# One query tile moved forward, and four smaller reorderings, in a two-layer hybrid decoder trunk

## The chip, the core and the metric

The kernel runs on one core of a Trainium2 chip. The metric is the device time of one execution in microseconds. The core has TensorE (PE, matrix products into PSUM banks), VectorE (DVE), ScalarE (ACT), GpSimd (POOL) and SyncE (SP), and DMA engines that are started from the queues of SP, ACT and POOL. Each engine works through its own instructions in order and waits on semaphores.

## The reference

A residual stream of 16 learned meta tokens and 512 tokens (528 columns, 1024 channels, float32) passes two layers. Per layer:

```
h = rmsnorm(x) * gain
u, z_pool, c_q, c_kv, k_rope, z_mla, g_pool, g_mla = split(h @ w_in)     # 512,512,768,256,32,512,1024,1024
y_pool = (pool_mix(u, w_group) * pool_scale * silu(z_pool)) @ pool_w_up  # causal means over 2,4,8,16 tokens, minus u
y_mla  = (attention(c_q, c_kv, k_rope) * silu(z_mla)) @ mla_w_up         # 8 heads, 64+32 wide, q/k norms, rotary part
x = x + (sigmoid(g_pool) * y_pool + sigmoid(g_mla) * y_mla) @ w_out
```

The meta columns are dropped from the output, so in the last layer most products run on 512 columns, in the first on 528 in two halves of 264.

## The kernel before

**Products.** All activations lie channel-major (channels on partitions, tokens in columns). Each float32 product is made of three reduced-precision ones: a weight tile `w` is split into `whi` (a ScalarE copy, L187) and `wlo` (a VectorE subtraction, L188), the activation into `hh` and `hl`, and `mm3` (L192, L195, L196) adds `whi*hh`, `whi*hl` and `wlo*hh` in one PSUM bank. There are four banks tagged `mm`, three tagged `S` and one `o`.

**The stream of products.** `register` writes down, layer by layer, the list `plan` of `Gemm`s; `stream` walks it in pieces of 512 weight columns (four 128-wide steps of the contraction). At each piece it asks `wload` for the next piece's weights: a DMA from SP's queue into `raw` (three buffers), then the two splits into rings of three (or, for tiles marked `spare`, two other buffers). When an output tile is complete its evacuation function (`ev_cq`, `ev_u`, `ev_o`, ...) takes it out of PSUM. The attention heads and norms are written between the pieces: `go` calls `fill`, `fill_now`, `upto`, which step the stream on by a modelled time (`clk`) or to a named product. `behind(a, b)` adds a dependency: `a` may not start before `b` has ended. `newest[0]` is the matmul last written down, `earlier(ns)` the one written `ns` nanoseconds of the modelled clock ago. The framework's scheduler then orders each engine's instructions by its own simulated timeline, so the order in the queues is near that of the program, but not the same.

**The order in a layer.** ckv0, ckv1 (key/value latent), then the norm's sums and its reciprocal root, which goes to memory and comes back broadcast as `inv` (`rinv<-ndr`). Meanwhile cq0 to cq4 run (query latent; they need no `inv`, `ev_cq` only sums squares into `racc` on POOL). Then u0, k0, u1, kr, k1, u2, k2, u3, k3 (pooled inputs and keys; `ev_u` and `ev_k` multiply by `inv` or `cinv`), v, then `yw`: the 512 columns of the pooled group weights, kept in two `sv` buffers for the four products y0 to y3. The rest alternates zp (pool gate) with y tiles as fillers: zp0, zp1, y0, zp2, y1, zp3, y2, cq5, y3; then qr0, qr1 (rope part of the queries, with a rotation on VectorE and POOL in `rope`), qn0 to qn3, pu, zm, the gates and the heads. `qr` and `qn` need all six cq tiles.

**Output.** After the products mu0 to mu7 the residual stream is read back into `xb` by eight DMAs of POOL (`residual`). o0, o1, o2 and o3 are plain products with w_out, 128 output channels each; `ev_o` adds half of the PSUM bank to `xb` on VectorE (L1092) and starts the tile's write (`out`, L1101; in the last layer to `yT`, from POOL's queue). The other four output tiles are computed in pairs with seven instead of eight half products, a Strassen-like scheme (`out_pairs`): group `oa` holds products 1, 2, 7, 6, 5 for two pairs, o3 follows, then group `ob` holds 4 and 3. VectorE prepares sums and differences of the activations (`blend`); sums of weight tiles were made in memory long before by plain and accumulating DMAs (`weight_sums`, L356 and L359). Some products are added to two outputs: `carry` (L1163, L1164) copies the bank to a buffer on ScalarE and adds it to `xb` by an accumulating DMA of POOL; the next product for the same bank accumulates on it, so it waits for that copy.

Of the kernel before, what the change touches and what calls it, by code (L numbers as in the profile page):

```python
# [10 lines left out]
F32R = mybir.dt.float32r  # L11
BF16 = mybir.dt.bfloat16
I32 = mybir.dt.int32
AF = mybir.ActivationFunctionType
ALU = mybir.AluOpType
# [7 lines left out]
NM = 16  # L23
# [49 lines left out]
def trunk(ctx, tc, xT, pos, win, wkr, wqb, wkb, wvb, wgr, wpu, wmu, wout, gains, const, yT):  # L73
# [17 lines left out]
    def slot(tag, dt=F32, bufs=1, w=W):  # L91
        return sl.tile([P, w], dt, tag=tag, name=nm(tag), bufs=bufs)

    def tmp(w=W):
        return tp.tile([P, w], F32, tag="tmp", name=nm("tmp"), bufs=3)
# [18 lines left out]
    def fetch(src, n, raw, eng):  # L114
        eng.dma_start(raw[:, :n], src)
        return raw

    def rawt():
        return wp.tile([P, 512], F32, tag="raw", name=nm("raw"), bufs=3)
# [49 lines left out]
            return self.src[c // 512] if isinstance(self.src, list) else self.src[:, c:c + n]  # L169

    loads = [0]

    def wload(src, n, gain, spare, buf=None, held=False):
        raw = early.pop(0) if early else fetch(src, n, buf or rawt(), sp)
        loads[0] += 1
        pool, th, tl, nb = (tp, "th", "tl", 2) if loads[0] <= 2 or spare else (wp, "whi", "wlo", 3)
        if gain is not None:
            v = raw[:, :n].rearrange("p (k m) -> p k m", k=8)
            gp.tensor_mul(v, v, gain.unsqueeze(2).to_broadcast([P, 8, n // 8]))
            return raw, None  # L180
        if held:
            hi, lo = slot("sv", F32R, bufs=2), slot("sv", F32R, bufs=2)
            split(hi, lo, raw[:, :n], 0, n)
            return hi, lo
        hi = pool.tile([P, W if pool is tp else 512], F32R, tag=th, name=nm("whi"), bufs=nb)
        lo = pool.tile([P, W if pool is tp else 512], F32R, tag=tl, name=nm("wlo"), bufs=nb)
        act.activation(hi[:, :n], raw[:, :n], AF.Copy)  # L187
        dve.tensor_sub(lo[:, :n], raw[:, :n], hi[:, :n].bitcast(F32))  # L188
        return hi, lo

# [10 lines left out]
    def earlier(ns):  # L201
        return next((m for c, m in reversed(past) if c <= clk[0] - ns), past[0][1])

    newest = [None]
    plan = []
# [96 lines left out]
    def split(hi, lo, src, a, b):  # L302
        act.activation(hi[:, a:b], src, AF.Copy)  # L303
        dve.tensor_sub(lo[:, a:b], src, hi[:, a:b].bitcast(F32))  # L304

    def behind(ins, other):
        tc.add_manual_dep(ins.ins, other.ins.name,
                          mybir.DependencyInfo(mybir.DependencyClass.Sync, mybir.DependencyReason.DATA))
# [38 lines left out]
    def weight_sums(name, w):  # L347
        def made(u, i):
            a, b = w[2 * u], w[2 * u + 1]
            d = wsum[name][u]  # L350
            src = {0: (b[:, 0:512], b[:, 512:1024]), 2: (a[:, 0:512], b[:, 0:512]), 1: (a[:, 0:512], d[:, 0, :]),
                   3: (a[:, 512:1024], d[:, 1, :])}
            return d[:, i, :], src[i]

        def copy(d, src):
            behind(sp.dma_start(d, src[0]), earlier(14000))  # L356

        def add(d, src):
            behind(gp.dma_start(d, src[1], accum_op=ALU.add), earlier(4000))  # L359

        for u in range(len(w) // 2):
            for fn, i in ((copy, 0), (copy, 2), (add, 0), (copy, 1), (add, 2), (add, 1), (copy, 3), (add, 3)):
                yield lambda fn=fn, u=u, i=i: fn(*made(u, i))

    class Layer:
# [723 lines left out]
        def ev_o(self, m, nxt):  # L1089
            def ev(ps, a, b):  # L1090
                x = xb[:, m, a:b]
                dve.scalar_tensor_tensor(out=x, in0=ps, scalar=0.5, in1=x, op0=ALU.mult, op1=ALU.add)  # L1092
                self.out(m, (a, b), nxt, gp)
                if not self.last and m == 3 and b == T:
                    nxt.square_x(m)
            return ev
# [46 lines left out]
        def out_pairs(self, nxt, name, products):  # L1143
            order = [(p, u) for p in products for u in range(2)]
            l = self.l
            a, b, c = self.halves()
            n = b - a
            A, B = (a, b), (b, c)
            src = []
            for p, u in order:  # L1150
                w0, w1 = wout[l, OUT[2 * u]], wout[l, OUT[2 * u + 1]]
                src.append({1: w0[:, 0:512], 2: w0[:, 512:1024], 4: w1[:, 512:1024]}.get(p))
                if src[-1] is None:
                    src[-1] = wsum[l][u][:, {5: 0, 6: 1, 7: 2, 3: 3}[p], :]
            bank = self.banks

            def grow(m, s, v):
                x = xb[:, m, s[0]:s[1]]
                dve.scalar_tensor_tensor(out=x, in0=v, scalar=0.5, in1=x, op0=ALU.mult, op1=ALU.add)

            def carry(m, s, v, u, scale, o):
                t = self.carried[u][:, o:o + n]
                act.activation(t, v, AF.Copy, scale=scale)  # L1163
                gp.dma_start(xb[:, m, s[0]:s[1]], t, accum_op=ALU.add)  # L1164

            def body(i, w):
                p, u = order[i]
                m0, m1 = OUT[2 * u:2 * u + 2]
                key = {2: "e", 7: "c", 4: "c"}.get(p, "a"), u
                if key not in bank:  # L1170
                    bank[key] = (sct if key[0] == "a" else mmt)()
                ps = bank[key][:, :n]
                t, o = (B if p == 3 else A), (0 if p == 1 else 4)
                for k in range(4):
                    xh, xl = (x[:, t[0]:t[1]] for x in self.mg[k + o]) if p < 4 else self.tt[k][p]
                    c_ = P * k
                    mm3(ps, w[0][:, c_:c_ + P], w[1][:, c_:c_ + P], xh, xl, k == 0 and p in (1, 2, 7), k == 3, True)
                    if k == 1:
                        yield 6 * (n / 2.4)
                q = sp if name == "ob" else gp  # L1180
                if p == 1:
                    self.carried[u] = slot("sv", bufs=2)
                    carry(m0, A, ps, u, 0.5, 0)
                elif p == 2:
                    grow(m0, A, ps)
                    self.out(m0, A, nxt, q)
                elif p == 7:
                    grow(m1, B, ps)
                elif p == 6:
                    carry(m1, A, ps, u, -0.5, HALF)  # L1190
                elif p == 5:
                    carry(m1, B, ps, u, -0.5, 0)
                    self.out(m1, B, nxt, q)
                    if u == 1 and not self.last:
                        for m in range(3):
                            nxt.square_x(m)
                elif p == 4:
                    grow(m1, A, ps)
                    self.out(m1, A, nxt, q)
                else:  # L1200
                    grow(m0, B, ps)
                    self.out(m0, B, nxt, q)
                    if not self.last:
                        nxt.square_x(m0)
                        nxt.square_x(m1)
                if i == len(order) - 1:
                    done.add((l, name))
                yield 6 * (n / 2.4)

            plan.append(Gemm((l, name), src, 512 * len(src), body=body))  # L1210
            plan[-1].more = True

        def register(self, nxt):
# [4 lines left out]
            def add(name, src, width, **kw):  # L1218
                plan.append(Gemm((l, name), src, width, **kw))
# [5 lines left out]
            def cq(m):  # L1225
                add(f"cq{m}", wi(MT_CQ + m), D, evac=self.ev_cq(m), xs=hs, segs=XS)
# [1 line left out]
            def kk(p):  # L1228
                add(f"k{p}", wkb[l, p], 256, evac=self.ev_k(p), xs=cs, segs=FULL)

            for m in range(5):
                cq(m)
            for m in range(4):
                add(f"u{m}", wi(MT_U + m), D, evac=self.ev_u(m), xs=hs, segs=FULL)
                if m == 1:
                    add("kr", wkr[l], 256, body=self.kr_body, gain=gn[:, l * N_GAIN + G_H:l * N_GAIN + G_H + 8])
                kk(m)
# [4 lines left out]
                add(f"y{m}", None, P, body=self.y_body(m))  # L1242

            add("v", wvb[l], 1024, body=self.v_body)
            add("yw", wgr[l], 512, body=self.hold)
            plan[-1].held = True
            zp(0)
            zp(1)
            y(0)
# [1 line left out]
            y(1)  # L1251
            zp(3)
            y(2)
            cq(5)
            y(3)
            for r in range(2):
                add(f"qr{r}", wqb[l, r], 768, evac=self.ev_qr(r), xs=lambda: self.cqs, segs=XS)
            for p in range(4):
                add(f"qn{p}", wqb[l, 2 + p], 768, evac=self.ev_qn(p), xs=lambda: self.cqs, segs=XS)
            for m in range(8):  # L1260
# [17 lines left out]
                add(f"mu{m}", wmu[l, m], 512, evac=self.ev_mu(m), xs=lambda: self.ogs, segs=XS)  # L1278
                plan[-1].spare = m % 2 == 1
            mg = lambda: self.mg  # L1280
            self.banks, self.carried = {}, {}
            for m in range(4):
                if m == 3:
                    self.out_pairs(nxt, "oa", (1, 2, 7, 6, 5))
# [165 lines left out]
```

## Time and profile before

| | |
|---|---|
| median of three runs | 781.85 us (781.79 to 782.32) |
| profiled execution | 781.9 us |
| its span, first to last instruction | 780.1 us |
| TensorE busy | 773.2 us, 5469 matmuls, full clock |
| VectorE busy | 569.7 us |
| ScalarE busy | 444.7 us |
| POOL busy | 232.7 us |

The span is 1.8 us shorter than the profiled execution's own time. A row of a timeline gives start and duration in microseconds, engine, source line, operation, output and inputs by the program's names, shape, count, and in brackets the engine's idle time before it with what ended it. A matmul's shown duration is longer than the step to the next start, because matmuls overlap. A row of a stage (from:to, its length) gives busy microseconds with instruction counts for PE, its weight loads, DVE, ACT and POOL, then the granted clock, the share of the 16 DMA engines and GB/s. A row of DMA issues gives target, source, queue, count, size and the median time from issue to landing.

### The profile page before, as it was taken

To read this page: it belongs to the slowest core of one execution; us is meant where nothing else is said; L and a number is where in the kernel's file an instruction comes from. 1 tells how busy PE (TensorE), PEld (TensorE's weight loads), DVE (VectorE), ACT (ScalarE), POOL (GpSimd) and SP (SyncE) were. 2 spreads that over 40 slices of the span, in tenths; PEclk is the share of its full clock that TensorE was granted. 3 is DMA by queue.
4 is the path that set the end of the run, shared out by engine and by line. 5 is a ranking of instruction groups with operands and counts; after the bars stand their busy time and mean duration, and the time that the engine had idled before them with its cause. 6 is when DMAs were issued, how large, how long until landed. Compare 5 with 4: busy or idle time off the path is not lost.

```text
span 780.1 us, 15325 instructions
## 1 busy us (share of the span) xinstructions
PE 773.2 (99%) x5469; PEld 710.9 (91%) x5469; DVE 569.7 (73%) x1326; ACT 444.7 (57%) x1016; POOL 232.7 (30%) x303
## 2 busy tenths in 40 slices
PE   9999999999999999999999999999999999999998
PEld 8999899999999999999997898887788999988887
DVE  5848787446778876589764577866897888864994
ACT  7645555645566665645564446546657766664552
POOL 1024525103335333211330136221006625340213
PEclk9999999999999999999999999999999999999999
DMA  6232457765646465565662424425557666662645
GB/s 245 82 96 89 125 171 151 177 168 144 156 110 164 116 141 120 156 156 184 169 171 82 109 75 122 133 62 178 146 132 167 173 187 158 175 226 72 210 137 154
DMA packets 65325, 112.92 MB, mean 145 GB/s; under 512 B 10704, under 2 KB 15696, under 8 KB 65248
## 3 DMA queue, kind: packets, MB, share of 16 engines
q1 hardware_dynamic: 55344, 92.18, 39.1%
q0 software_dynamic: 8896, 17.92, 12.9%
q10 hardware_dynamic: 1008, 1.84, 0.7%
q8 instruction: 43, 0.70, 0.4%
q14 instruction: 34, 0.28, 0.1%
HBM read 100.18 MB, written 22.62 MB: 157 GB/s over the span
## 4 chain that ended last, share of the span: by engine, by line
PE 91%; DVE 4%; DMA 2%; ACT 1%; issue 1%; POOL 0%; DVEq 0%; ACTq 0%; POOLq 0%
PE mm L192 26%; PE mm L196 26%; PE mm L195 25%; PE S L195 3%; PE S L196 3%; PE S L192 3%; PE mm L979 2%; DVE wlo L188 1%; PE o L985 1%; PE o L984 1%; PE S L506 1%; DMA raw<-wgr 1%; DMA xb<-xT 1%; PE mm L408 1%; ACT whi L187 0%
## 5 line engine op out<-in xcount | busy, mean ns | idle before, releaser
L192 PE MATMUL mm<-hh,whi 128*128 128x264 f32 (+2 forms) x992 | 306.2, 311 | 0.5 <-DVE u L550 0.4
L196 PE MATMUL mm<-hh,wlo 128*128 128x264 f32 (+2 forms) x992 | 304.4, 309 | 0.1
L195 PE MATMUL mm<-hl,whi 128*128 128x264 f32 (+2 forms) x992 | 304.1, 308 | 0.0
L188 DVE TENSOR_TENSOR wlo<-raw,whi 128x512 fp32r<-128x512 f32 (+1 forms) x253 | 180.0, 714 | 100.3 <-ACT whi L187 98.0
L187 ACT ACTIVATE whi<-raw 128x512 fp32r<-128x512 f32 (+1 forms) x253 | 154.2, 613 | 168.7 <-PE mm L195 110.2
L192 PEld LDWEIGHTS mm<-hh,whi 128*128 128x128 f32 x992 | 186.2, 188 | 11.3 <-issue 1.0
L195 PEld LDWEIGHTS mm<-hl,whi 128*128 128x128 f32 x992 | 186.8, 188 | 8.7
L196 PEld LDWEIGHTS mm<-hh,wlo 128*128 128x128 f32 x992 | 185.9, 188 | 9.0 <-DVE wlo L188 0.6
L922 POOL TENSOR_SCALAR pa<-pa,rs 128x272 f32<-128x272 f32 (+1 forms) x32 | 33.2, 1038 | 103.3 <-DVE rs L941 64.5
L922 POOL TENSOR_SCALAR cq<-cq,rs 128x400 f32<-128x400 f32 (+1 forms) x32 | 51.2, 1600 | 0.0
L192 PE MATMUL mm<-cq,whi 128*128 128x264 f32 (+2 forms) x140 | 43.8, 313 | 0.0
L195 PE MATMUL mm<-cq,whi 128*128 128x264 f32 (+2 forms) x140 | 43.7, 312 | 0.0
L196 PE MATMUL mm<-cq,wlo 128*128 128x264 f32 (+2 forms) x140 | 43.3, 312 | 0.1
L908 DVE CUSTOM_DVE_ANT_0 S<-S,maskw,nqs 128x272 f32<-128x272 f32 (+4 forms) x80 | 38.6, 498 | 5.3 <-PE S L196 5.0
L725 POOL TENSOR_TENSOR racc<-racc,tmp 128x264 f32<-128x264 f32 (+1 forms) x15 | 14.0, 936 | 85.5 <-ACT tmp L724 85.5
L304 DVE TENSOR_TENSOR tl<-mm,th 128x512 fp32r<-128x512 f32 (+1 forms) x64 | 30.0, 483 | 8.0 <-ACT th L303 6.3
L359 POOL DMA_DIRECT2D wsum<-wout x8 | 7.0, 875 | 91.6 <-PE mm L196 86.9
L303 ACT ACTIVATE th<-mm 128x512 fp32r<-128x512 f32 (+1 forms) x64 | 26.3, 433 | 10.2 <-PE mm L979 9.6
L915 ACT ACTIVATE cq<-S,bia 128x400 f32<-128x400 f32 (+2 forms) x48 | 24.5, 514 | 13.2 <-DVE bia L953 8.5
L192 PE MATMUL mm<-u,whi 128*128 128x264 f32 (+1 forms) x96 | 31.3, 326 | 0.0
L196 PE MATMUL mm<-u,wlo 128*128 128x264 f32 (+1 forms) x96 | 30.9, 322 | 0.0
L195 PE MATMUL mm<-kn,whi 128*128 128x264 f32 (+1 forms) x96 | 30.6, 320 | 0.0
(344 smaller groups left out, 1684.7 us busy)
## 6 DMA issues: line engine op xcount, KB each, us to landing
raw<-win SPq DMA_DIRECT2D x139, 256.0 KB, 2.8
raw<-wout SPq DMA_DIRECT2D x22, 256.0 KB, 3.6
bc<-kdr SPq DMA_DIRECT2D x16, 264.0 KB, 4.5
wsum<-wout SPq DMA_DIRECT2D x16, 256.0 KB, 3.5
raw<-wpu SPq DMA_DIRECT2D x16, 256.0 KB, 2.7
wsumgp<-win SPq DMA_DIRECT2D x16, 256.0 KB, 3.4
raw<-wmu SPq DMA_DIRECT2D x16, 256.0 KB, 2.8
raw<-wsumgp SPq DMA_DIRECT2D x16, 256.0 KB, 4.3
```

The costliest lines, as they stand in the source:

```text
L187: act.activation(hi[:, :n], raw[:, :n], AF.Copy)
L188: dve.tensor_sub(lo[:, :n], raw[:, :n], hi[:, :n].bitcast(F32))
L192: first = pe.matmul(out, wh, xh, start=start, stop=False, skip_group_check=more)
L195: pe.matmul(out, wh, xl, start=False, stop=False, skip_group_check=more)
L196: newest[0] = pe.matmul(out, wl, xh, start=False, stop=stop, skip_group_check=more)
L303: act.activation(hi[:, a:b], src, AF.Copy)
L304: dve.tensor_sub(lo[:, a:b], src, hi[:, a:b].bitcast(F32))
L725: self.acc_last = gp.tensor_add(self.acc[:, a:b], self.acc[:, a:b], t[:, :b - a])
L908: dve.tensor_tensor_reduce(out=sv, in0=sv, in1=mask, scale=nqs[:, i, h:h + 1], scalar=3e38, op0=ALU.add, op1=ALU.min, accum_out=bia[:, c:c ...
L915: act.activation(pv, sv, AF.Exp, scale=-1.0, bias=bia[:, i:i + 1], accum_out=rs[:, c:c + 1])
L922: gp.tensor_scalar(pt[i], pt[i], rs[:, i:i + 1], None, op0=ALU.mult)
L979: pe.transpose(tr[:, P * (i - j):P * (i - j + 1)], pt[i][:, NM + P * j:NM + P * (j + 1)], ident)
```

## The change

Five edits in one:

1. `register`: cq5 goes in front of u0, behind cq4. Its former place between y2 and y3 is taken by qr0; qr1 follows y3.
2. `register` and `wload`: `yw` goes from behind v to behind u2 (ahead of k2). Its load takes a buffer of the tag `bc` (three, otherwise used by the heads for broadcast rows) in place of one of the three `raw` buffers, and waits for the matmul last written down.
3. `wload` and `carry`: a ScalarE split of a weight tile that is the second or third one written down after a `carry` may not start before that carry's copy.
4. `ev_o` in the last layer, for o0, o1 and o2: in place of the VectorE addition, a ScalarE copy with factor 0.5 into a `tmp` buffer and an accumulating DMA of POOL into `xb`. The write to `yT` is put off: it is written down after the first product of group `ob`, on SP's queue, behind that product's last matmul.
5. `weight_sums`: the accumulating DMAs wait for a matmul 9000 ns back on the modelled clock, not 4000.

```
 loads = [0]
+urgent = []

 def wload(src, n, gain, spare, buf=None, held=False):
+    if held:
+        hi, lo = slot("sv", F32R, bufs=2), slot("sv", F32R, bufs=2)
+        raw = slot("bc", bufs=3)
+        behind(sp.dma_start(raw[:, :n], src), newest[0])
+        split(hi, lo, raw[:, :n], 0, n)
+        return hi, lo
     raw = early.pop(0) if early else fetch(src, n, buf or rawt(), sp)
...
-    if held:
-        hi, lo = slot("sv", F32R, bufs=2), slot("sv", F32R, bufs=2)
-        split(hi, lo, raw[:, :n], 0, n)
-        return hi, lo
...
-    act.activation(hi[:, :n], raw[:, :n], AF.Copy)
+    made = act.activation(hi[:, :n], raw[:, :n], AF.Copy)
+    for e in urgent:
+        e[1] += 1
+        if 1 < e[1] < 4:
+            behind(made, e[0])
     dve.tensor_sub(lo[:, :n], raw[:, :n], hi[:, :n].bitcast(F32))

 def add(d, src):                                  # in weight_sums
-    behind(gp.dma_start(d, src[1], accum_op=ALU.add), earlier(4000))
+    behind(gp.dma_start(d, src[1], accum_op=ALU.add), earlier(9000))

 def ev(ps, a, b):                                 # in ev_o
     x = xb[:, m, a:b]
+    if self.last and m < 3:
+        t = tmp()[:, a:b]
+        act.activation(t, ps, AF.Copy, scale=0.5)
+        gp.dma_start(x, t, accum_op=ALU.add)
+        self.later.append(lambda: behind(sp.dma_start(yT[:, m, a - NM:b - NM], x), newest[0]))
+        return
     dve.scalar_tensor_tensor(out=x, in0=ps, scalar=0.5, in1=x, op0=ALU.mult, op1=ALU.add)

 def carry(m, s, v, u, scale, o):                  # in out_pairs
-    act.activation(t, v, AF.Copy, scale=scale)
+    urgent.append([act.activation(t, v, AF.Copy, scale=scale), 0])
     gp.dma_start(xb[:, m, s[0]:s[1]], t, accum_op=ALU.add)
...
+    while self.later and name == "ob":            # in body, after the product's additions
+        self.later.pop(0)()

-for m in range(5):                                # in register
+for m in range(6):
     cq(m)
 for m in range(4):
     add(f"u{m}", ...)
+    if m == 2:
+        add("yw", wgr[l], 512, body=self.hold)
+        plan[-1].held = True
     if m == 1:
         add("kr", ...)
     kk(m)
...
 add("v", wvb[l], 1024, body=self.v_body)
-add("yw", wgr[l], 512, body=self.hold)
-plan[-1].held = True
...
 y(2)
-cq(5)
+qr(0)
 y(3)
-for r in range(2):
-    add(f"qr{r}", ...)
+qr(1)
```

More of the change, by code (lines that the diff above doesn't have):

```diff
@@ L1253, in register, with qr @@
             y(2)
-            cq(5)
-            y(3)
-            for r in range(2):
-                add(f"qr{r}", wqb[l, r], 768, evac=self.ev_qr(r), xs=lambda: self.cqs, segs=XS)
+            def qr(r):
+                add(f"qr{r}", wqb[l, r], 768, evac=self.ev_qr(r), xs=lambda: self.cqs, segs=XS)
+            qr(0)
+            y(3)
+            qr(1)
             for p in range(4):
@@ L1280, in register @@
             mg = lambda: self.mg
-            self.banks, self.carried = {}, {}
+            self.banks, self.carried, self.later = {}, {}, []
             for m in range(4):
```

## The prediction

> **What bounds the kernel now.** I read the page's head, then the work by stage (busy microseconds of each engine in a stretch, instruction counts in brackets, granted clock, DMA share and GB/s).
>
> ```profile
> span 780.1 us, 15325 instructions
> PE 773.2 (99%) x5469; PEld 710.9 (91%) x5469; DVE 569.7 (73%) x1326; ACT 444.7 (57%) x1016; POOL 232.7 (30%) x303
> 75.00:90.00 15.00, 14.59 (x104) 12.72 (x106) 12.70 (x25) 9.69 (x24) 13.05 (x12) 1.00 0.43 141
> 720.00:757.00 37.00, 36.01 (x180) 30.08 (x178) 35.11 (x72) 19.91 (x42) 5.51 (x10) 1.00 0.51 164
> 772.70:777.40 4.70, 4.21 (x36) 4.00 (x35) 1.70 (x4) 0.00 (x0) 1.08 (x2) 1.00 0.66 196
> ```
>
> TensorE (PE) is busy 773.2 of 780.1 us at full clock, and the change neither adds nor removes a matmul. So nothing that makes another engine faster counts by itself: the end can only move by the holes in TensorE's stream, or by what follows its last matmul. Holes are read from the timeline of PE by the step from one start to the next, since a matmul's shown duration overlaps its successor.
>
> ```profile
> 57.97 0.28 PE L195 MATMUL mm<-kl,whi 128*128 128x264 f32 x1
> 58.09 0.28 PE L196 MATMUL mm<-kh,wlo 128*128 128x264 f32 x1
> 58.80 0.36 PE L192 MATMUL mm<-hh,whi 128*128 128x264 f32 x1 [0.42 <-DVE u L550]
> 83.35 0.39 PE L195 MATMUL mm<-wlo,kh 128*128 128x512 f32 x1
> 83.58 0.40 PE L196 MATMUL mm<-whi,kl 128*128 128x512 f32 x1
> 84.38 0.50 PE L192 MATMUL mm<-whi,kh 128*128 128x512 f32 x1 [0.41 <-DVE u L550]
> 476.03 0.40 PE L196 MATMUL mm<-whi,kl 128*128 128x512 f32 x1
> 476.48 0.50 PE L192 MATMUL mm<-whi,kh 128*128 128x512 f32 x1
> 531.85 0.40 PE L195 MATMUL mm<-cq,whi 128*128 128x512 f32 x1
> 532.33 0.50 PE L196 MATMUL mm<-cq,wlo 128*128 128x512 f32 x1
> 755.73 0.28 PE L196 MATMUL mm<-hh,wlo 128*128 128x256 f32 x1
> 757.08 0.39 PE L192 MATMUL S<-cq,whi 128*128 128x256 f32 x1 [1.07 <-ACT sv L1163]
> ```
>
> An undisturbed step is 0.12 us for 264 columns (57.97 to 58.09) and 0.23 for 512 (83.35 to 83.58); for 256 columns I also use 0.12. The holes are then 0.71 - 0.12 = 0.59 us at 58, 0.80 - 0.23 = 0.57 at 84, 0.45 - 0.23 = 0.22 at 476, 0.48 - 0.23 = 0.25 at 532, and 1.35 - 0.12 = 1.23 at 756. All five lie in stages that the change touches. The first four edits reach the holes at 58, 84, 476 and 756: 0.59 + 0.57 + 0.22 + 1.23 = 2.61 us is what they can win there.
>
> **The sixth query-latent tile (cq5) before u0.** Who made the hole at 58? SyncE's queue and the engines behind it:
>
> ```profile
> 42.15 0.37 SPq L115 DMA_DIRECT2D raw<-win  x1
> 49.03 0.33 SPq L444 DMA_DIRECT2D rinv<-ndr  x1
> ndr<-ny SPq DMA_DIRECT2D x4, 2.0 KB, 8.4
> 52.54 0.63 ACT L187 ACTIVATE whi<-raw 128x512 fp32r<-128x512 f32 x1 [5.10 <-DMA raw<-win]
> 57.41 0.90 DVE L188 TENSOR_TENSOR wlo<-raw,whi 128x512 fp32r<-128x512 f32 x1 [1.04 <-ACT whi L187]
> 58.23 0.76 DVE L550 TENSOR_TENSOR u<-mm,rinv 128x264 f32<-128x264 f32 x2
> ```
>
> The norm row goes to memory and back, and its four scattered writes take 8.4 us to land. SyncE stands until 49.03 behind them, and the weight tile issued at 42.15 reaches ScalarE only at 52.54, after 5.10 us of idleness. From then on ScalarE and VectorE work off cq4's evacuation and the splits late, and u0's evacuation at 58.23 sits behind a split: TensorE wants u0's PSUM bank for u1 after the short k0. This backlog made the hole. With cq5 in front, 48 more matmuls, 48 x 0.12 = 5.8 us, stand between the late tile and u0; they need cq4's banks no sooner than u0 did, and only cq5 follows, not a short k tile. I take the whole 0.59 as won. What covers the delayed group (all of u, k, kr, v moves back by 5.8 us) is that same tile; nothing outside waits for it before the heads. In the second layer no hole stands at this place, so I count nothing there.
>
> Between y2 and y3 the place of cq5 goes to qr0 (18 matmuls a column half, against 24), so y3 comes nearer to its pooled input; but in layer one y3's operand (window 3) is made long before, and qr0's operands are now old. I cost the filler itself at nothing. What it does to VectorE is below.
>
> **The pooled weights (yw) early, through buffers of their own.** The holes at 84 and 476 have one cause:
>
> ```profile
> 79.42 0.33 SPq L115 DMA_DIRECT2D raw<-wgr  x1
> 82.32 0.63 ACT L303 ACTIVATE sv<-raw 128x512 fp32r<-128x512 f32 x1 [2.28 <-DMA raw<-wgr]
> 82.98 1.00 DVE L304 TENSOR_TENSOR sv<-raw,sv 128x512 fp32r<-128x512 f32 x1 [0.85 <-ACT sv L303]
> 83.91 0.42 DVE L550 TENSOR_TENSOR u<-mm,rinv 128x264 f32<-128x264 f32 x1
> ```
>
> ScalarE waits 2.28 us for this load, VectorE another 0.85 behind ScalarE, and u3's evacuation, next in VectorE's order, frees the bank only after 83.91. After the change the load needs no free buffer of the ring of three; it starts after a matmul in the middle of u2 and lands, by the same 2.9 us (79.42 to 82.32), about when u2's second half ends. The split can still hold ScalarE and VectorE for a moment, but what is then late is k2's bank, which is wanted only a whole u tile later (5.8 us). SyncE's queue is passed by one wait on a matmul; behind it are the weights for k2 and u3, two buffers ahead. I take 0.57 + 0.22 as won, at worst half of it.
>
> **The last layer's o0 to o2, and the order of the splits behind the carries.** The hole at 756:
>
> ```profile
> 750.66 0.68 DVE L1092 SCALAR_TENSOR_TENSOR xb<-mm,xb 128x512 f32<-128x512 f32 x1
> 755.42 0.68 DVE L188 TENSOR_TENSOR wlo<-raw,whi 128x512 fp32r<-128x512 f32 x1
> 756.12 0.63 ACT L187 ACTIVATE whi<-raw 128x512 fp32r<-128x512 f32 x1 [1.57 <-PE mm L196]
> 756.66 0.64 ACT L1163 ACTIVATE sv<-S 128x256 f32<-128x256 f32 x2
> xb<-sv POOLq DMA_DIRECT2D x6, 128.0 KB, 3.5
> yT<-xb POOLq DMA_DIRECT2D x4, 256.0 KB, 3.4
> ```
>
> Both carries (756.66) were behind a split that ScalarE waited 1.57 us to start; TensorE needed them, because the next product accumulates on the bank they read. VectorE is full here (35.11 of 37.00 us in the stage), so the splits of the pair products are late too. The change takes three 0.68 us additions off VectorE (2.04 us) and gives ScalarE, busy 19.91 of 37.00, three copies of about 0.63 (the row of a 512-wide ScalarE pass). It also lets the second and third split after a carry start only behind it. Upper end: all 1.23. Lower end: the split of 756.12 ends at 756.75, and its product cannot start before: 757.08 - 756.75 = 0.33 is then all there is. I take 1.0, near the upper end, since VectorE's 2.04 us come before that split's raw buffer was freed. In layer one the carry edit meets no hole; I cost it at nothing, as a split is made two to three chunks ahead, each of 12 matmuls of 0.12 us.
>
> The three additions become accumulating DMAs of 256 KB; half that size takes 3.5 us to land, and nobody reads these tiles until the end, 20 us on. Three writes of the result move from POOL's queue to SyncE's, behind the first product of the last group, at about 773: 768 KB more in the last 4.7 us, where the DMA engines now are at 0.66 and 196 GB/s. At that share the stage could carry 196 / 0.66 = 297 GB/s, an estimate, so 0.34 x 4.7 x 297 = 0.47 MB fit into the idle share and 0.3 MB, about 1.0 us, do not. Bounds 0 and 1.0; I take 0.1, because the last write's issue is the latest of all and most of the excess has drained by the landing. [...]
>
> **The weight sums (9000 for 4000).** Each accumulating DMA of the sums waits for a matmul some 5 us older. POOL issues them sooner and blocks less; the copy it needs waits for a matmul 14000 ns back and is written down two tasks before it. No hole lies there. Nothing, plus or minus 0.1.
>
> **qr0, y3, qr1 on VectorE.** In layer two the hole at 532 comes from VectorE beside POOL's rope:
>
> ```profile
> 512.00 0.43 DVE L188 TENSOR_TENSOR wlo<-raw,whi 128x256 fp32r<-128x256 f32 x1 [0.40 <-ACT whi L187]
> 517.70 1.25 DVE L304 TENSOR_TENSOR tl<-tmp,u 128x512 fp32r<-128x512 f32 x1 [0.70 <-ACT u L303]
> 528.44 1.53 DVE L188 TENSOR_TENSOR wlo<-raw,whi 128x256 fp32r<-128x256 f32 x1
> 527.88 1.81 POOL L541 TENSOR_TENSOR q<-q,tc 128x512 f32<-128x512 f32 x1 [1.29 <-DVE tmp L835]
> ```
>
> The same 256-wide split takes 0.43 us with POOL idle and 1.53 with the rope running. y3's evacuation (a 512-wide pass of 0.68 and the split, 1.25 beside POOL) now falls between two ropes: 1.9 us of VectorE against y3's three matmuls of 0.23. Bounds: the hole of 0.25 goes (y3 parts the ropes), or 1.9 - 0.7 = 1.2 us come on top. I take 0.1 lost: most of these operations have no near deadline.
>
> Sum: 0.59 + 0.57 + 0.22 + 1.0 - 0.1 - 0.1 = 2.18 us. The profiled execution took 781.9 us (its span of 780.1 and 1.8 around it), the median of the runs is 781.85; the forecast is 781.9 - 2.2 = **779.7 us**. A difference of 0.2%, 1.56 us, is about what a measurement of this kernel can tell from no change.
>
> **Rivals.** *The end hole stays.* For it: ScalarE's split at 756.12 waits on TensorE, and the weights behind it are loaded only when VectorE frees raw buffers. Then 0.33 is won in place of 1.0, and the tail may cost up to 1.0: 2.18 - 0.67 = 1.5 without the tail, 0.6 with it, so 780.4 to 781.3. Against: VectorE's relief. No measurable change.
>
> *VectorE and POOL collide around qr0.* 1.2 us lost for 0.1 gives 2.18 - 1.1 = 1.1 won, 780.8 us; if layer one, where no hole stands now, pays the same again, nothing is won: 781.9. [...]
>
> *Slower: SyncE's queue stops in the last group.* The three result writes wait for the first product of the last group; in the program's order the loads of its third and fourth weight tiles come after them.
>
> ```profile
> 764.94 0.33 SPq L115 DMA_DIRECT2D raw<-wsum  x1
> 773.41 4.32 SPq L1101 DMA_DIRECT2D yT<-xb  x4
> ```
>
> If the load of 764.94 came behind them, at about 773.4, then with 3.4 us to land (as the 256 KB write above) and 0.63 + 0.68 of splitting its product would start at 778.1. Now the last write's issue ends at 773.41 + 4.32 = 777.73, some 0.8 us behind the last product, and two products of 12 x 0.12 = 1.44 us end there, so the third starts at about 774.1: 4.0 us lost, and with the 2.2 won 783.7 us. It decides only if the load stands behind the writes. Against: now, too, this load precedes a write (773.41) that the program issues before it, so SyncE's order goes by readiness. A new order elsewhere with holes of that size belongs to the same case.
>
> *The change does not do what it says*: the splits and loads keep their order and 781.9 stays; part of the second case.
>
> **How the numbers follow.** Forecast case 0.62, its own range 778.6 (2.61, the 0.25 at 532, and some 0.1 us for each of the four slow first matmuls after a hole, such as 0.50 for 0.39) to 780.3. End hole stays 0.13 and collision or no effect 0.12, up to 781.9: within 0.2% together 0.25. Slower 0.13. The range 778.6 to 782.0 leaves out the slower case and little else.
>
> **What would show it.** Right: no step over 0.2 us before the matmul that follows k0, none in v's first products, and the first S product of group oa within 0.4 us of its predecessor; ScalarE's wait for wgr under 0.5 us. Wrong: a wait of SyncE before the last raw load, a split of over 1.5 us between qr0 and qn0 with a hole behind it, or over 3.2 us from the last addition's end to the end of the span.

## The result, and the profile after

The changed kernel took 786.6 us (median of 13 runs, 782.55 to 788.54); the kernel before, beside it, 782.62 us (13 runs, 781.72 to 783.95). The ratio is 1.0041, with a 95% interval of 1.0029 to 1.0052: 0.4% slower, where 0.3% faster was forecast. The changed kernel's times spread more than those of before, and with TensorE's mean granted clock: three runs at 1.000 took 782.55 to 783.69 us, the ten at 0.997 to 0.999 took 784.32 to 788.54. The profiled execution took 786.6 us.

The head of the page and the work by stage of the changed kernel. The first stage is that of the prediction, with 5 us more for the work that now comes later; the second holds the work that lay at 720 to 757 before, 4.0 us later now:

```profile
span 784.4 us, 15328 instructions
PE 774.5 (99%) x5469; PEld 712.3 (91%) x5469; DVE 568.7 (73%) x1323; ACT 446.5 (57%) x1019; POOL 229.4 (29%) x303
75.00:95.00 20.00, 20.00 (x152) 18.20 (x152) 18.60 (x38) 12.31 (x30) 13.85 (x13) 1.00 0.35 109
724.00:761.00 37.00, 36.88 (x183) 30.45 (x182) 34.45 (x71) 20.81 (x45) 8.09 (x13) 1.00 0.59 166
```

The span is 4.3 us longer. In the early stage TensorE now has no gap (20.00 of 20.00), and in the second VectorE has 34.45 us of work for 35.11: 0.7 less, not 2.04, since other work has come in. The holes that the prediction named look like this now (timeline of PE, start and shown duration):

```profile
64.04 0.28 PE L203 MATMUL mm<-kh,wlo 128*128 128x264 f32 x1
64.16 0.28 PE L199 MATMUL mm<-hh,whi 128*128 128x264 f32 x1
89.05 0.40 PE L203 MATMUL mm<-whi,kl 128*128 128x512 f32 x1
89.28 0.39 PE L199 MATMUL mm<-whi,kh 128*128 128x512 f32 x1
758.23 0.28 PE L203 MATMUL mm<-hh,wlo 128*128 128x256 f32 x1
758.61 0.39 PE L199 MATMUL mm<-hh,whi 128*128 128x256 f32 x1
764.78 0.28 PE L202 MATMUL S<-u,whi 128*128 128x256 f32 x1
765.33 0.38 PE L203 MATMUL S<-cq,wlo 128*128 128x256 f32 x1 [0.27 <-DVE wlo L195]
```

Behind k0 the step to u1 is 0.12 us, in v's first products 0.23: those holes are gone, as are the ones at 476 and 532. The hole of 1.23 at 756 has become 0.38 - 0.12 = 0.26 us, one of 0.17 right behind it, and 0.55 - 0.12 = 0.43. So of the five holes that the prediction read four are gone, and of the fifth 0.37 us is won where 1.0 was forecast. The loss is elsewhere, in layer one, ahead of the products mu, where the prediction had not looked:

```profile
332.75 0.28 PE L203 MATMUL mm<-hh,wlo 128*128 128x264 f32 x1
335.93 0.51 PE L199 MATMUL mm<-q,whi 128*128 128x264 f32 x2 [2.90 <-ACT q L310]
337.25 0.42 PE L199 MATMUL mm<-q,whi 128*128 128x264 f32 x1
337.46 0.42 PE L202 MATMUL mm<-kn,whi 128*128 128x264 f32 x1
332.77 1.15 ACT L190 ACTIVATE whi<-raw 128x512 fp32r<-128x512 f32 x2 [3.66 <-DMA raw<-wmu]
333.43 1.29 DVE L195 TENSOR_TENSOR wlo<-raw,whi 128x512 fp32r<-128x512 f32 x2 [3.60 <-ACT whi L190]
328.00:336.00 8.00, 5.10 (x42) 4.84 (x40) 3.49 (x10) 2.74 (x9) 0.00 (x0) 1.00 0.57 133
336.00:340.00 4.00, 4.00 (x21) 4.00 (x22) 2.76 (x11) 1.77 (x5) 0.00 (x0) 0.57 0.48 151
```

Read from the bracket backwards: TensorE stood for 2.90 us, because ScalarE stood for 3.66 us until a load of mu's weights landed, and VectorE for 3.60 behind ScalarE; the operands of the next products stand in their queues behind the splits of those weights. The step is 3.18 us, 3.06 of it lost. Behind the hole the granted clock is 0.57 on average over 4 us, and a matmul step is 0.21 to 0.23 us in place of 0.12: another 0.43 x 4 = 1.7 us. These 4.8 us and some smaller holes, less what was won, are the longer span. The largest of the smaller ones are new too, in layer two (0.46 us at 668.6 and 0.80 at 670), and begin in the same way, with ScalarE behind a load (in the kernel before it stood 0.48 us at this place):

```profile
667.90 0.63 ACT L190 ACTIVATE whi<-raw 128x512 fp32r<-128x512 f32 x1 [2.29 <-DMA raw<-win]
```

The load for which ScalarE stood in layer one, on the chain of work that ended last, before and after (start, then time to landing):

```profile
328.35 2.55 DMA raw<-wmu
327.30 5.38 DMA raw<-wmu
```

It takes 2.83 us longer, which is what the hole has grown by (3.06 for 0.23 at 333.8 before). What delays it is seen in POOL's queue, before (L359) and after (L366), from the second of three in a row:

```profile
329.27 0.81 POOL L359 DMA_DIRECT2D wsumgp<-win  x1 [8.68 <-PE mm L196]
330.14 0.83 POOL L359 DMA_DIRECT2D wsumgp<-wsumgp  x1
323.35 0.81 POOL L366 DMA_DIRECT2D wsumgp<-win  x1 [2.31 <-PE mm L203]
326.75 0.83 POOL L366 DMA_DIRECT2D wsumgp<-wsumgp  x1 [2.58 <-DMA wsumgp<-win]
```

These accumulating DMAs go out 5.9 and 3.4 us sooner, some 1.0 us of it because everything here lies that much earlier. At 5.7 us to landing (below) both now run beside the load of 327.30; before, the load of 328.35 had landed at 330.9, soon after they were issued. That is the fifth edit, the one that the prediction put at nothing.

### The profile page after: what moved, and what is told of

Same layout as the page of the kernel before. It is cut to its first block, busy times and chain, and to the rows that moved or that the text cites. A ratio compares the mean times of both kernels' runs of the same rounds, so it can differ in the third digit from the quotient of the medians.

```text
span 784.4 us, 15328 instructions
## 1 busy us (share of the span) xinstructions
PE 774.5 (99%) x5469; PEld 712.3 (91%) x5469; DVE 568.7 (73%) x1323; ACT 446.5 (57%) x1019; POOL 229.4 (29%) x303
## 4 chain that ended last, share of the span: by engine, by line
PE 94%; DMA 2%; DVE 2%; ACT 1%; issue 0%; SPq 0%; DVEq 0%; ACTq 0%
PE mm L199 27%; PE mm L203 26%; PE mm L202 26%; PE S L202 2%; PE S L203 2%; PE S L199 2%; PE mm L986 2%; PE o L992 1%; PE o L991 1%; DMA xb<-xT 1%; PE S L513 1%; DMA raw<-wmu 1%; DVE wlo L195 1%; PE mm L415 1%; DMA raw<-win 1%; PE mm L472 0%
## 5 line engine op out<-in xcount | busy, mean ns | idle before, releaser
L195 DVE TENSOR_TENSOR wlo<-raw,whi 128x512 fp32r<-128x512 f32 (+1 forms) x253 | 182.2, 723 | 106.1 <-ACT whi L190 103.8
L929 POOL TENSOR_SCALAR pa<-pa,rs 128x272 f32<-128x272 f32 (+1 forms) x32 | 31.2, 975 | 98.1 <-DVE rs L948 59.6
L199 PE MATMUL mm<-q,whi 128*128 128x264 f32 (+1 forms) x96 | 30.5, 329 | 2.9 <-ACT q L310 2.9
L366 POOL DMA_DIRECT2D wsum<-wout x8 | 6.9, 865 | 87.0 <-PE mm L203 72.0
```

The lines of the kernel that those rows point to most:

```text
L199: first = pe.matmul(out, wh, xh, start=start, stop=False, skip_group_check=more)
L929: gp.tensor_scalar(pt[i], pt[i], rs[:, i:i + 1], None, op0=ALU.mult)
```

## The experiments

The theory after the traces: the fifth edit puts accumulating DMAs beside weight loads that have no slack, and a long hole lowers the clock (2.90 us of idle time in TensorE, then 0.57 over 4 us). The rivals: the shift of everything by the first two edits, or the third and fourth edit.

**e1_all_but_adds and e2_adds_alone.** The changed kernel without the fifth edit, and the fifth edit alone:

```
-behind(gp.dma_start(d, src[1], accum_op=ALU.add), earlier(9000))
+behind(gp.dma_start(d, src[1], accum_op=ALU.add), earlier(4000))
```

> All edits but the fifth: the weight sums' accumulating DMAs wait for a matmul 4000 ns old again. Theory (the fifth edit lets two accumulating DMAs run beside the loads of mu's weights, which are then late, and the 3 us hole that follows lowers TensorE's clock): no hole over 0.3 us at about 333, no split that waits 3.66 us for its load, clock 1.00 throughout; the time is 782.6 less the holes won (0.59 + 0.57 + 0.22 + 0.25 + 0.8) = 780.2, up to 781.9 if the new holes at 668 and 383 stay. Rival (cq5 and yw move all that follows by about 1 us, and this brings the load into the hole): hole and low clock stay, 786 us.

> The kernel before with 9000 for 4000 and nothing else. Theory: a hole of 2 to 3 us before mu in layer one and a clock of 0.5 for some 3 us behind it: 782.6 + 3.06 - 0.23 + 1.7 = 787.1 us. Rival (the shift by the other edits is needed): no new hole, 782.6 within 0.5 us.

Without the fifth edit: 782.82 us, ratio to before 1.0008 (0.9999 to 1.0017), the hole at 333 is 0.25 us and the clock 1.00. That is 2.6 to 3.8 us better than the whole change (by the ratios 0.33%, by the medians 3.8), but outside the 780.2 to 781.9 that were expected. The fifth edit alone: 784.74 us, 1.0032 (1.0021 to 1.0043), between the two expectations (787.1, and 782.6 within 0.5). Its hole ahead of mu is smaller than in the changed kernel, 1.39 us with the clock at 1.00:

```profile
334.78 0.28 PE L196 MATMUL mm<-hh,wlo 128*128 128x264 f32 x1
336.29 0.51 PE L192 MATMUL mm<-q,whi 128*128 128x264 f32 x2 [1.24 <-ACT q L303]
```

ScalarE stood 2.00 us for the load there. The hole in layer two is here as well (1.10 us at 668.8, ScalarE 2.06 us behind a load), and one of 0.81 at 146.9, for which the profile names a matmul and not a load. Against the shift as rival: the fifth edit loses with and without the other edits. But e1 is no faster than before, where the first four edits should have won 2.2 us, so one of these loses too.

**e3_cq_yw and e4_last.** The first two edits alone, and the third and fourth alone (diffs as in the change).

> The kernel before with the first two edits (cq5 ahead of u0, qr0 as filler, yw early). By the prediction: the holes at 58, 84, 476 and 532 go, 782.6 - 0.59 - 0.57 - 0.22 - 0.25 = 781.0 us, and nothing new comes. Rival of the shift: the hole at 333 is there, and with the low clock 786 us or more. Holes at 668 that are new here would be the price of the moved products in the second layer.

> The kernel before with the third and fourth edit alone (splits behind the carries, o0 to o2 added by DMA, their writes later on SyncE's queue). By the prediction: 1.0 won at 756, 0.1 lost at the end, 782.6 - 0.9 = 781.7 us. By the changed kernel's trace a hole of 0.43 behind the first S product and two of 0.26 and 0.18 remain: 0.4 won, 782.2. If the later writes of the result are what costs: 783 us or more, all of it behind the last product.

The first two: 780.81 us, 0.9985 (0.9974 to 0.9996), 1.2 us won by the ratio, 1.65 by the medians, and all four holes at 58, 84, 476 and 532 are gone. For the one at 58 that proves little: it is missing in e2 and e4 too, which have no first edit. Behind k0 in e2:

```profile
58.29 0.28 PE L196 MATMUL mm<-kh,wlo 128*128 128x264 f32 x1
58.41 0.28 PE L192 MATMUL mm<-hh,whi 128*128 128x264 f32 x1
```

The weight tile that was late reached ScalarE at 51.62 in e2 and 51.53 in e4, at 52.54 in the profile of before. So this hole seems to come and go with that load, and how much of its 0.59 us the first edit won is not shown. The other three stand in e2 and e4 and are gone only with the first two edits.

The third and fourth: 784.13 us, 1.0023 (1.0014 to 1.0033), slower. One alternative had 783 us or more, but all of it behind the last product; the hole is in group oa (PE, then VectorE):

```profile
762.21 0.28 PE L200 MATMUL S<-u,whi 128*128 128x256 f32 x1
763.98 0.39 PE L201 MATMUL S<-cq,wlo 128*128 128x256 f32 x1 [1.49 <-DVE wlo L193]
762.30 0.42 DVE L1170 SCALAR_TENSOR_TENSOR xb<-mm,xb 128x256 f32<-128x256 f32 x1 [2.82 <-PE S L201]
762.64 0.68 DVE L193 TENSOR_TENSOR wlo<-raw,whi 128x512 fp32r<-128x512 f32 x1
```

VectorE stood 2.82 us before an addition, with the split that TensorE wanted next behind it. The profile names a matmul as releaser, but the addition reads `xb` too, into which the carries' accumulating DMAs run: those of this stretch took 6.5 us to land (3.9 in e7, below). I took this for the work of the fourth edit's accumulating DMAs. The next two experiments show that these do not do it alone.

**e6_cq_yw_carry and e7_cq_yw_odma.** The first two edits and the third; the first two and the fourth.

> The first three edits (e3_cq_yw measured 780.8). Theory (the third edit lets the carries go first, but bunches three splits behind them): the hole of 1.14 before the first S product becomes two of 0.26 and 0.18, and two of 0.23 and 0.17 are new in layer one's group: 780.8 - 1.14 + 0.84 = 780.5 us, no 1 us hole at about 760. Rival (the third edit also makes the hole of 0.4 to 1.6 at 762 that follows in the changed kernels): 781.0 to 782.0.

> The first, second and fourth edit. Theory (three accumulating DMAs of 256 KB at 748 to 755 slow the weight loads and the carries' own accumulating DMAs; VectorE's additions wait for these with the next split behind them): holes of 1 to 2 us in all between 750 and 763, the last write 0.4 us later: 780.8 - 1.14 + 2 + 0.4 = 782.1, within 1 us. Prediction's own step (three additions less on VectorE close the hole): 780.8 - 1.0 + 0.1 = 779.9 us.

With the third: 782.85 us, 1.0007 (0.9997 to 1.0016), that is 0.22% or 1.7 us worse than e3 by the ratios, worse than either expectation. With the fourth: 781.11 us, 0.9981 (0.9972 to 0.9990), as good as e3; the hole at 756 is gone without a trace, and no hole over 0.25 us lies behind 670. The time by itself settles nothing: it is at the edge of my theory's range (782.1 within 1 us) and 1.2 us above the 779.9 of the prediction's step. But the holes of my theory are not there. VectorE's last three splits of `raw` ahead of the old hole start at 749.82, 751.09 and 753.97 in e3 and at 750.66, 752.27 and 754.21 in e7, where the same work otherwise lies 2.0 us later: 0.8 to 1.8 us earlier against TensorE's stream. So my theory on the fourth edit fell, and the prediction's own step for it held. What it wins there is mostly given back at the end: from the last addition to the end e7 takes 3.49 us, before 2.70. What the third does is seen on ScalarE, in e3 (first two rows) and e6:

```profile
754.59 0.63 ACT L189 ACTIVATE whi<-raw 128x512 fp32r<-128x512 f32 x1 [1.48 <-PE mm L198]
755.13 0.64 ACT L1165 ACTIVATE sv<-S 128x256 f32<-128x256 f32 x2
753.88 0.66 ACT L1170 ACTIVATE sv<-S 128x256 f32<-128x256 f32 x2
754.42 0.63 ACT L190 ACTIVATE whi<-kl 128x512 fp32r<-128x512 f32 x1
754.94 0.63 ACT L190 ACTIVATE whi<-raw 128x512 fp32r<-128x512 f32 x1
755.46 0.63 ACT L190 ACTIVATE whi<-kh 128x512 fp32r<-128x512 f32 x1
757.44 1.29 ACT L190 ACTIVATE whi<-raw 128x512 fp32r<-128x512 f32 x2 [1.34 <-DMA raw<-wsum]
```

The carries (`sv`) do go ahead of the split behind which they stood in e3. But in ScalarE's order 260 of the 268 splits lie ahead of this first pair of carries in e3, and 255 in e6: five went behind it, three of them in a row. TensorE takes the products as their splits are made (0.26 us at 754.7, 0.18 at 755.3), and ScalarE waits 1.34 us for a load that was issued at 751.91, behind the VectorE split that freed its buffer, and took 5.50 us to land. That the held splits free their buffers late and so make the loads late is my reading: e7 has a wait of 1.30 us for such a load too, and no hole. The hole of 1.14 us has become 0.26 + 0.18 + 0.12 + 0.50 us, with 0.40 ahead of them. In layer one, where there was no hole, the same edit makes two; the first of them:

```profile
378.69 0.28 PE L203 MATMUL mm<-hh,wlo 128*128 128x264 f32 x1
379.04 0.39 PE L199 MATMUL mm<-hh,whi 128*128 128x264 f32 x1
```

The first is 0.35 - 0.12 = 0.23 us, the second, 0.22 us on, is 0.18. With the last group these rows make 0.7 us of the 1.7; the rest is not located, and lies within what the two intervals leave open. They stand at this place in e1, e4, e5, e6 and the changed kernel, and not in e2, e3, e7 or before: only the kernels with the third edit have them. The 762 hole of e4 is in e1 and the changed kernel too (0.91 and 0.43), but not in e6 or e7: it takes the third and fourth edit together. Why the carries' DMAs land so late only then is not shown.

**e8_third_only.** A milder third edit:

```
-if 1 < e[1] < 4:
+if e[1] == 3:
```

> As e6_cq_yw_carry, but only the third split after a carry has to wait for it, not the second. Theory: the carries still go first, the splits behind them are less bunched: the hole of 1.14 becomes under 0.5 us and layer one's two small holes go, 780.8 - 0.8 = 780.0 us. Rival (the order of the splits is as good as before whichever is held): within 0.3 us of e6_cq_yw_carry.

781.82 us, 0.9994 (0.9985 to 1.0003): layer one's holes are gone, but the hole in the last group is 0.26 + 0.61 + 0.48 + 0.18 us, more than the 1.14 of e3. I expected 780.0, or within 0.3 us of e6; by the ratios it is 1.0 us better than e6 and 0.7 worse than e3, and the latter is within the uncertainty. That holding even one split costs the time of its raw buffer is my reading and not shown by itself.

**e5_half_adds and e10_eighth_adds.** Is it the bytes of the accumulating DMAs? The changed kernel, with half and with an eighth of them (the rest of the sums is left out):

```
-behind(gp.dma_start(d, src[1], accum_op=ALU.add), earlier(9000))
+behind(gp.dma_start(d[:, 0:256], src[1][:, 0:256], accum_op=ALU.add), earlier(9000))   # e10: 0:64
```

> The changed kernel, but each accumulating DMA of the weight sums moves only the first 256 of its 512 columns (the other half of the sums is left out). Waits, queues and order stay. Theory (these DMAs take the DMA engines from the loads of mu's weights): the hole at 333 falls from 3.06 to under 1 us, ScalarE's wait for the load from 3.66 to under 1.7 us, the clock stays at 1.00, and the time goes from 786.6 to 786.6 - 2.5 - 1.7 = 782.4 us. Rival (the place of the adds in the queues and their semaphores make the hole, whatever they move): hole, low clock and 786 us stay.

> As e5_half_adds, but each accumulating DMA of the weight sums moves 64 of its 512 columns (the rest of the sums is left out). Theory (the bytes count: whole 3.06, half 1.65, none at that place 0.24): a hole of 0.24 + 2.82 / 8 = 0.6 us at 333, the load of mu's weights within 3 us, 782.8 us as without the fifth edit. Rival (half of the hole is the DMAs' fixed cost or their place): the hole stays at 1.4 to 1.7 us and the time at 783.4.

783.42 us (1.0019, 1.0008 to 1.0029) and 781.73 us (0.9994, 0.9985 to 1.0003). The hole at 333, and the DMA issues between 318 and 334 us (size each, median from issue to landing) of the changed kernel, of e5 and of e10:

```profile
raw<-wmu SPq DMA_DIRECT2D x4, 256.0 KB, 4.6
wsumgp<-win POOLq DMA_DIRECT2D x2, 256.0 KB, 5.7
raw<-wmu SPq DMA_DIRECT2D x6, 256.0 KB, 4.0
wsumgp<-win POOLq DMA_DIRECT2D x2, 128.0 KB, 3.3
334.38 0.51 PE L199 MATMUL mm<-q,whi 128*128 128x264 f32 x2 [1.49 <-ACT q L310]
raw<-wmu SPq DMA_DIRECT2D x7, 256.0 KB, 2.7
wsumgp<-win POOLq DMA_DIRECT2D x2, 32.0 KB, 2.5
334.20 0.51 PE L199 MATMUL mm<-q,whi 128*128 128x264 f32 x2 [0.24 <-ACT q L310]
```

The waits and queues are the same in all three; the weight load goes from 4.6 to 4.0 to 2.7 us, the hole from 3.06 to 1.65 to 0.41, with whole, half and an eighth of the bytes; kernels without the fifth edit have up to 0.40 here (e3). Half was expected to bring it under 1 us and did not, so the first expectation missed; an eighth was put at 0.6. The bytes beside the load make the hole. That is shown for this place; for the other holes of the fifth edit it is read from the traces alone, and at 670 the holes do not follow the bytes (0.80 whole and 1.29 in e11, 0.19 with half, 0.59 with an eighth, up to 0.51 without the edit).

**e9_writes_earlier.** e7, with the three late writes of the result one group earlier:

```
-while self.later and name == "ob":
+while self.later and i == len(order) - 1:
```

> As e7_cq_yw_odma, but the three late writes of the result are written down behind the last product of group oa, not behind the first of group ob, so that they may go out some 7 us before the end. Theory (the fourth edit closes the hole at 756, as predicted, and gives 0.8 back behind the last product, because 768 KB of writes crowd the last 5 us): from the last matmul to the end of the span 3.5 less 0.8 = 2.7 us, as in the kernel before; 781.1 - 0.8 = 780.3 us, the best so far. Rival (the last write's own 1.7 to 2.1 us sets the end, whatever is beside it): 781.1 within 0.3 us.

779.91 us, 0.9969 (0.9957 to 0.9981): the fastest kernel here, 0.31% under the kernel before and below the changed one by 0.72%. From the last addition to the end e7 takes 3.49 us, e9 3.05, before 2.70, so the writes explain some 0.4 us, half of what was expected; the rest of the 1.2 us between the medians of e7 and e9 lies within what the two intervals leave open.

**e11_changed_again.** The changed kernel, a second profile.

> The changed kernel once more, unaltered, for a second profile of its variable place. Theory (the hole's length depends on how the DMAs fall in each execution, and the low clock follows only a long one): with a hole under 2 us the clock is 1.00 and the run takes 784 us or less; with one of 3 us there are again some 3.4 us at 0.5, and 786 us or more. Rival (the hole is fixed): again 3.06 us and 786 to 787.

787.47 us; the hole at 333 is 3.53 us this time, and again the clock falls:

```profile
335.93 0.79 PE L199 MATMUL mm<-q,whi 128*128 128x264 f32 x2 [3.36 <-ACT q L310]
336.00:340.00 4.00, 4.00 (x21) 4.00 (x22) 2.75 (x11) 1.76 (x5) 0.00 (x0) 0.58 0.46 141
```

That hole and clock vary together is not shown by it, as this execution fell on the long side; that the low clock goes with holes of 3.06 and 3.53 us, and not with 1.65 (e5) or 1.39 (e2), behind which the matmul step stays at 0.11 to 0.14 us, is.

## Why the prediction was wrong, point by point

By the ratios, the parts are: first and second edit -1.2 us (e3), third +1.7 (e6 against e3), fourth -0.3 (e7 against e3), fifth +2.6 (the whole change against e1). Their sum is +2.8, the whole change +3.2 (0.41% of 782.4); each part is uncertain by about 1 us.

- *cq5 and yw: right for yw, open for cq5.* 0.59 + 0.57 + 0.22 were claimed, and the holes are gone in every kernel with these edits. The 0.25 at 532, counted only for the range, went too. But the 0.59 was read from a single profile, and the hole is also missing in two kernels that keep cq5 where it was (e2, e4): it should have been taken with a chance.
- *qr0, y3, qr1: right.* The splits beside POOL's rope in layer two are slow, as the collision rival said (two 256-wide ones took 3.22 us together at 530.7; before, one took 0.43 with POOL idle), but no hole stands behind them in any of these kernels.
- *VectorE's relief closes the hole at 756: right for the fourth edit.* e7 and e9 have no hole there, so all of 1.23 was to be had from it. In the whole change only 0.37 was, because the third edit and its meeting with the fourth opened holes beside it.
- *"In layer one the carry edit meets no hole; I cost it at nothing, as a split is made two to three chunks ahead": wrong.* This step priced where the carry gets ahead and not what it puts behind: five splits move behind the first pair of carries, three of them bunch, and TensorE waits for them. It lost 1.7 us (e6 against e3), 0.4 of them in layer one. The part that their buffers play is not shown.
- *The tail: mis-sized.* 0.1 us was taken, between 0 and 1.0; behind the last addition the changed kernel takes 3.10 us for 2.70, so 0.4, and e7 3.49, so 0.8 (over the 3.2 that was named as a sign of being wrong).
- *"No hole lies there. Nothing, plus or minus 0.1": the step that cost most, 2.6 us.* Without it the change makes no measurable difference (e1); with it, it is slower. It looked for holes that the earlier adds could close. It did not ask beside which loads the DMAs would now run, and whether those have slack. The trace of before held both answers; its row at that load already had ScalarE waiting:

```profile
330.98 1.16 ACT L187 ACTIVATE whi<-raw 128x512 fp32r<-128x512 f32 x2 [0.82 <-DMA raw<-wmu]
```

So this load had no slack. The accumulating DMAs take 5.7 us each to land (median); two of them moved onto it, it took 5.38 us for 2.55, and ScalarE's wait went from 0.82 to 3.66 us: 2.84 more for a load that took 2.83 longer.
- *The slower rival* named another place: SyncE's queue did not stop, the last load was issued at 768.74 and the first write at 776.85. Its last sentence, a new order elsewhere with holes of that size, is what happened, and the chance of 0.13 for it was too small for a change of five edits, of which two had been priced at nothing without a look at the transfers around them.

## What to carry to other kernels

Price a moved DMA by what it will run beside: list the loads in flight at its new time and read, in the wait of the engine that uses them, whether they have any slack. Where instructions are held back so that another may go first, price what waits for the held ones, and not only what gets ahead: here three splits in a row were bunched behind the carries, and the edit lost 1.7 us (e6 against e3). Where several edits come in one change, each needs its own row, and the parts are worth trying apart: here the first, second and fourth edit, with the writes moved earlier, beat both kernels.

## What the runs showed of the hardware

Byte for byte, the accumulating DMAs took 2.4 times the DMA engines' time of the plain ones. Between 321 and 335 us of the changed kernel (queue: packets, MB, share of the 16 engines' time; q0 holds POOL's accumulating DMAs, q1 the plain ones of SyncE):

```profile
q0 software_dynamic: 432, 0.79, 47.6%
q1 hardware_dynamic: 445, 0.80, 19.7%
```

For as many bytes that is 47.6 / 19.7 = 2.4 times the engines' time. POOL's queue by itself does not show it: between 700 and 735 us, where it holds plain copies alone (`xb<-scr`), its share is 7.9% for 0.85 MB and that of q1 28.5% for 3.11 MB, 9.3 and 9.2% per MB. Nor does writing to memory: of the copies with the same source and target in the whole changed kernel, the plain ones (SyncE) land in 3.5 us and the accumulating ones (POOL) in 6.2 (medians):

```profile
wsumgp<-win SPq DMA_DIRECT2D x16, 256.0 KB, 3.5
wsumgp<-win POOLq DMA_DIRECT2D x8, 256.0 KB, 6.2
```

The hole at 333 cost more than its length. In both profiles of the changed kernel the clock was low (0.57 and 0.58 on average from 336 to 340 us) behind a stretch in which TensorE was idle for 2.90 and 3.36 us. By single microseconds from 335 on, the granted clock of the first profile is 1.00, 0.72, 0.50, 0.50, 0.58 and 1.00: half of full speed for some 3.4 us, an estimate from these numbers (0.28 + 0.50 + 0.50 + 0.42 = 1.70 us lost, at 0.50 for each microsecond), and it fell some 0.5 us after the matmuls had begun again at 335.93. In e5 and e2, where TensorE was idle for 1.49 and 1.24 us at this place, the matmul step behind it is 0.11 to 0.14 us; from how long an idle time on the clock falls is not shown.
